# Low parts, copies and gate units of the first block given to other engines and places, and identity matmuls put ahead of five norms

## The chip, the cores and the metric

One core of a Trainium2 chip runs the whole program. The metric is device time in microseconds (us) for one execution, as the median of several runs. The engines are TensorE (PE in the profile; its weight loads are PEld), VectorE (DVE), ScalarE (ACT), GpSimd (POOL) and SyncE (SP), which here issues the DMAs of the weights. Each engine works through its own instructions in the order in which they stand in the program, and waits where an operand or a buffer is not ready.

## The reference

Input x is 256 rows of 1024 columns. A first block mixes the rows by three kinds of attention and a gated merge, and has a feed-forward part; two layers of a second block follow. What the change touches lies in the first block's mixing part and at the norms:

```python
h = rmsnorm(x, mix_norm_g[l])
proj = h @ w_in[l]
qa, ka, va, qd, kd, vd, qm, graw = jnp.split(proj, split_at, axis=-1)
heads = lambda t, n: t.reshape(B, S, n, HEAD_DIM)
qa = rope(rmsnorm(heads(qa, N_MOBA_HEADS), moba_q_norm_g[l]), positions)
ka = rope(rmsnorm(heads(ka, N_MOBA_HEADS), moba_k_norm_g[l]), positions)
...
gates = jax.nn.sigmoid(graw.astype(jnp.float32)).astype(x.dtype).reshape(B, S, N_BRANCHES, D_MODEL)
mem_n = rmsnorm(mem, mem_norm_g[l])
mkv = (mem_n @ w_mem_kv[l]).reshape(B, N_MEM, 2, N_MEM_HEADS, HEAD_DIM)
...
o_a = moba_attention(qa, ka, va).reshape(B, S, MOBA_W) @ w_branch_moba[l]
o_d = dilated_attention(qd, kd, vd).reshape(B, S, DIL_W) @ w_branch_dil[l]
o_m = memory_attention(qm, mk, mv).reshape(B, S, MEM_W) @ w_branch_mem[l]
merged = gates[:, :, 0] * o_a + gates[:, :, 1] * o_d + gates[:, :, 2] * o_m
x = x + merged @ w_out[l]
h2 = rmsnorm(x, ffn_norm_g[l])
...
```

Each layer of the second block has two more such norms, one ahead of its own input product and one ahead of the expert part: `h = rms_norm(x, norm1_g[l])` and `h2 = rms_norm(x, norm2_g[l])`.

## The kernel before

**Products.** Every large product is made of three: each operand is split into a high part, rounded to TensorE's fp32r format, and a low part, the rest; high x high, high x low and low x high are added up. `wload` (L88) brings one 128-row piece of a weight, a *unit*, into the chip: a DMA into `raw` (four buffers), a ScalarE copy that rounds it to `hi` (L102), and a subtraction that gives the *low part* `lw` (L103); `hi` and `lw` have three buffers each. On which engine the low part runs is set by `lo_on`: a pattern of engines, taken in turn, unit by unit. `gemm_n_unit` (L175 to L190) multiplies one unit: for each of the two halves t of the rows, L187 (high x high), L188 (high x low) and L190 (low x high). That is 12 matmuls of 128x512 for a unit of 1024 columns and 6 for one of 512. The sums stand in four accumulators `acc`; other results of TensorE go to four `tmp` buffers.

**Norms.** `norm_T` (L153) sums the squares of the rows, works out the factor of each row, scales the rows (L158 on ScalarE, L159 on VectorE), transposes them in 16 pieces of 128x128 on TensorE (L165) and splits each transposed tile (L111 on ScalarE, L112 on VectorE). Five norms come right behind a product whose sums they need: `ffn` in the first block (about 280 us), and `n1` and `n2` in either layer of the second (about 480, 615, 1435 and 1570 us). In these the first row of the list of products stands still until norm, transposes and first splits are done.

**The mixing part of the first block** runs from the start to 280 us. In the program's order:

- `w_in` in column groups for the heads, into `pj`, then the norm of `mem` and the product with `w_mem_kv` (eight units of 512 columns, low parts by turns on VectorE and GpSimd), into `kv`.
- `head_norm` and `rope_pair` on VectorE for the heads in `pj` (L429 to L452). `rope_pair` does, for each of two halves of the rows and two groups of six heads, six operations of 192 elements.
- The 24 units of the gates (three times 1024 columns, eight units each) are kept in a list `fill`. Two of them stand ahead of the first `head_T`, one is put behind each step of the attention rounds, and what is left stands at the end. All their low parts are on GpSimd (`lo_on(GP)`).
- `head_T` (L454) transposes the heads, four pieces to a `tmp` buffer (L460), and copies the result into `qkT`, by turns on ScalarE (L464) and VectorE (L466).
- The attention rounds (`run_pairs`, L296): scores (L233), a row maximum and a softmax on VectorE and ScalarE, transposes, products with the values.
- The branches: for each of three, a product of the attention's output with `w_branch` (3, 3 and 2 units), then for each quarter of the result a gated product on VectorE (L533) and, from the second branch on, an add into `merged` (L536). `merged` is transposed (L544), split, and multiplied with `w_out` (eight units). Low parts are on GpSimd here too.

A scheduler sets the order on each engine from the order in the code, with `high_priority` drawing instructions forward, and `tc.issue_after` holding one back until another has been issued.

## Time and profile before

| | |
|---|---|
| median of 3 runs | 2402.12 us (2401.92 to 2405.55) |
| profiled execution | 2397.52 us, its span 2395.7 us |
| TensorE busy | 2292.6 us, 96% of the span |
| VectorE busy | 1611.9 us, 67% |
| ScalarE busy | 1240.3 us, 52% |
| GpSimd busy | 675.1 us, 28% (275 of its 279 operations are low parts) |
| mean granted clock of TensorE | 0.974 of full speed |

In the rows further below, an operation is written as line, engine, kind, result <- operands, shape. Square brackets or the last column give the idle time of the engine ahead of it and what ended that. The granted clock is the share of TensorE's full speed (2.4 GHz) that it was given in a stretch; the values 0.50 and 0.51 are the lower level, 1.2 GHz.

### The profile page before, as it was taken

The page shows a single profiled execution, that of the slowest core. Times are in us where ns is not written, and L with a number is a line of the kernel's source. Part 1 is how long each engine was busy: PE and PEld are TensorE (multiplying, and loading weights), DVE is VectorE, ACT ScalarE, POOL GpSimd, SP SyncE. Part 2 cuts the span into 40 slices and gives each one's busy share as a digit, 9 for nine tenths or more (in the row PEclk, how much of TensorE's full clock was granted, in tenths as well). Part 3 has the DMA queues.
Part 4 walks back from the last instruction along what each step waited for, and adds up shares of the span by engine and source line. Part 5 has one row for each costly group of instructions (what it writes and reads, how often), then busy time and mean ns, then how long its engine had stood idle before and what let it go on. Part 6 is the DMA issues. An engine that isn't in the chain of part 4 may idle for free. (4 is left out here: it accounts for less than half of the span.)

```text
span 2395.7 us, 37317 instructions
## 1 busy us (share of the span) xinstructions
PE 2292.6 (96%) x13972; PEld 2000.6 (84%) x13972; DVE 1611.9 (67%) x3269; ACT 1240.3 (52%) x1997; POOL 675.1 (28%) x279
## 2 busy tenths in 40 slices
PE   7799899989999999999999998999999999999998
PEld 6578688777898999998888877889899999888886
DVE  7832577767597667776666667759766777666665
ACT  5444466545444555555555544544455555555553
POOL 3436444334576111220000004468512122000000
PEclk9899899989999999999999998999999999999999
DMA  6424355524454555446666653445455555666664
GB/s 205 137 80 149 130 181 192 168 86 136 158 168 151 167 160 176 165 162 194 193 194 193 194 175 94 136 157 169 151 166 160 167 174 163 192 194 194 193 193 149
DMA packets 111934, 393.07 MB, mean 164 GB/s; under 512 B 13432, under 2 KB 14328, under 8 KB 111496
## 3 DMA queue, kind: packets, MB, share of 16 engines
q1 hardware_dynamic: 108288, 384.42, 50.6%
q10 hardware_dynamic: 3464, 6.26, 0.8%
q8 instruction: 110, 1.80, 0.3%
q14 instruction: 72, 0.59, 0.1%
HBM read 389.58 MB, written 1.05 MB: 163 GB/s over the span
## 5 line engine op out<-in xcount | busy, mean ns | idle before, releaser
L103 POOL TENSOR_TENSOR lw<-raw,hi 128x1024 fp32r<-128x1024 f32 (+1 forms) x275 | 674.9, 2459 | 1357.5 <-ACT hi L102 1159.4
L102 ACT ACTIVATE hi<-raw 128x1024 fp32r<-128x1024 f32 (+1 forms) x748 | 778.0, 1040 | 442.5 <-PE tmp L205 188.1
L103 DVE TENSOR_TENSOR lw<-raw,hi 128x1024 fp32r<-128x1024 f32 (+2 forms) x473 | 573.2, 1214 | 219.0 <-ACT hi L102 218.5
L204 PE MATMUL tmp<-th,hi 128*128 128x256 f32 x1696 | 494.6, 292 | 5.2 <-DVE th L112 3.3
L206 PE MATMUL tmp<-th,lw 128*128 128x256 f32 x1696 | 484.3, 286 | 9.8 <-POOL lw L103 9.8
L187 PE MATMUL acc<-hi,th 128*128 128x512 f32 x1248 | 491.0, 394 | 2.7 <-ACT pj L374 2.4
L188 PE MATMUL acc<-lw,th 128*128 128x512 f32 x1248 | 490.2, 393 | 2.6 <-POOL lw L103 1.9
L205 PE MATMUL tmp<-th,hi 128*128 128x256 f32 x1696 | 483.8, 285 | 0.3
L213 PE MATMUL tmp<-th,hi 128*128 128x512 f32 x1136 | 411.4, 399 | 0.9 <-DVE th L112 0.9
L190 PE MATMUL acc<-hi,th 128*128 128x512 f32 x1248 | 393.4, 391 | 0.0
L206 PEld LDWEIGHTS tmp<-th,lw 128*128 128x128 f32 x1696 | 327.4, 193 | 11.1 <-POOL lw L103 10.6
L204 PEld LDWEIGHTS tmp<-th,hi 128*128 128x128 f32 x1696 | 327.6, 193 | 8.0 <-DVE th L112 5.0
L205 PEld LDWEIGHTS tmp<-th,hi 128*128 128x128 f32 x1696 | 328.0, 193 | 1.2 <-DVE th L112 0.7
L187 PEld LDWEIGHTS acc<-hi,th 128*128 128x128 f32 x1248 | 235.8, 189 | 53.6 <-ACT pj L374 2.8
L188 PEld LDWEIGHTS acc<-lw,th 128*128 128x128 f32 x1248 | 236.1, 189 | 53.1 <-POOL lw L103 2.7
L215 PE MATMUL tmp<-th,lw 128*128 128x256 f32 x994 | 279.8, 281 | 0.0
L190 PEld LDWEIGHTS acc<-hi,th 128*128 128x128 f32 x1248 | 235.5, 189 | 49.6 <-issue 0.7
L111 ACT ACTIVATE th<-W 128x256 fp32r<-128x256 f32 x252 | 104.4, 419 | 284.5 <-PE acc L188 284.5
L213 PEld LDWEIGHTS tmp<-th,hi 128*128 128x128 f32 x1136 | 213.2, 189 | 41.8 <-DVE th L112 1.3
L215 PEld LDWEIGHTS tmp<-th,lw 128*128 128x128 f32 x994 | 188.9, 190 | 1.9
L112 DVE SCALAR_TENSOR_TENSOR th<-W,th 128x256 fp32r<-128x256 f32 x252 | 106.2, 424 | 111.5 <-PE acc L190 111.4
L982 DVE TENSOR_TENSOR tmp<-tmp,pb 128x256 f32<-128x256 f32 x98 | 42.4, 432 | 150.2 <-ACT pb L981 149.9
(339 smaller groups left out, 2472.1 us busy)
## 6 DMA issues: line engine op xcount, KB each, us to landing
raw<-in_u_dram SPq DMA_DIRECT2D x256, 512.0 KB, 3.7
raw<-in_v_dram SPq DMA_DIRECT2D x256, 512.0 KB, 3.5
raw<-in_w_up_dram SPq DMA_DIRECT2D x44, 512.0 KB, 3.6
raw<-in_w_in_dram SPq DMA_DIRECT2D x40, 512.0 KB, 3.5
raw<-in_w2t_dram SPq DMA_DIRECT2D x32, 512.0 KB, 3.9
raw<-in_wq_dram SPq DMA_DIRECT2D x32, 512.0 KB, 3.5
raw<-in_w_out_dram SPq DMA_DIRECT2D x24, 512.0 KB, 3.4
raw<-in_w_down_dram SPq DMA_DIRECT2D x22, 512.0 KB, 3.6
```

The costliest lines, as they stand in the source:

```text
L102: SC.activation(hi[:, :ncols], r, AF.Copy)
L103: lo.tensor_sub(lw[:, :ncols], r, hi[:, :ncols].bitcast(F32))
L111: SC.activation(hi, ps, AF.Copy, scale=scale)
L112: V.scalar_tensor_tensor(lo, ps, scale, hi.bitcast(F32), op0=ALU.mult, op1=ALU.subtract)
L187: PE.matmul(ps, lh, wh[:, sl], start=first, stop=False)
L188: PE.matmul(ps, lh, wl[:, sl], start=False, stop=False)
L190: PE.matmul(ps, ll, wh[:, sl], start=False, stop=last)
L204: PE.matmul(ps, wh[:, sl], ah[:, c, :], start=(c == 0), stop=False)
L205: PE.matmul(ps, wh[:, sl], al[:, c, :], start=False, stop=False)
L206: PE.matmul(ps, wl[:, sl], ah[:, c, :], start=False, stop=(c == KC - 1))
L213: PE.matmul(ps, wh[:, sl], a2[:, c].rearrange("p a b -> p (a b)"), start=(c == 0), stop=(c == KC - 1))
L215: PE.matmul(ps[:, :S], wl[:, sl], a2[:, c, 0], start=False, stop=False)
```

## The change

1. `keep_going(n)` is new: n matmuls of the 128x128 identity with a 128x512 view of itself (bf16) into one `tmp` buffer, the first bound by `issue_after` to the last L190 of the product before. The five norms named above call it with 18. Nothing reads what they write.
2. Low parts: on VectorE alone for `w_mem_kv`, for the first six gate units, for the branches and for `w_out`; by turns on VectorE and GpSimd for the other gate units.
3. `rope_pair` takes both halves of the rows in one operation: six operations of 384 elements for each group of heads.
4. `head_T` copies on ScalarE alone.
5. Six gate units, not two, ahead of the first `head_T`.
6. The branches' adds come behind all four gated products of a branch, and each takes both halves of the rows (128x2x512).

```diff
--- before.py
+++ after.py
@@ -150,7 +150,17 @@
                 V.scalar_tensor_tensor(y, r, 1.5, y, op0=ALU.add, op1=ALU.mult)
         return [c[3] for c in cols], sq
 
-    def norm_T(src, scratch, g, hi, lo):
+    def keep_going(n):
+        ps = tmp_tile().rearrange("p (a b) -> p a b", a=4)
+        wide = identb[:, None].to_broadcast([128, 4, 128])
+        with tc.issue_after(hold["mm"].ins):
+            PE.matmul(ps, identb, wide, start=True, stop=True)
+        for _ in range(n - 1):
+            PE.matmul(ps, identb, wide, start=True, stop=True)
+
+    def norm_T(src, scratch, g, hi, lo, spins=0):
+        if spins:
+            keep_going(spins)
         with tc.high_priority(offset=150):
             rstd, sq = row_rstd(src, scratch)
             for h in range(2):
@@ -187,7 +197,7 @@
                     PE.matmul(ps, lh, wh[:, sl], start=first, stop=False)
                     PE.matmul(ps, lh, wl[:, sl], start=False, stop=False)
                 for ps, sl in grp:
-                    PE.matmul(ps, ll, wh[:, sl], start=False, stop=last)
+                    hold["mm"] = PE.matmul(ps, ll, wh[:, sl], start=False, stop=last)
 
     def gemm_n(units, ncols, ah, al, order=None, pre=()):
         nh = (ncols + 511) // 512
@@ -382,6 +392,7 @@
 
         mh = ab.tile([128, KC, S], F32R, name="mh", tag="mh")
         ml = ab.tile([128, KC, S], F32R, name="ml", tag="ml")
+        lo_on(V)
         norm_T(mem, xn, P("mem"), mh, ml)
         accs = gemm_n([A["w_mem_kv"][c * 128:(c + 1) * 128, :] for c in range(KC)], 512, mh, ml)
         evac_pj(accs, 0, 512, kv)
@@ -436,20 +447,19 @@
                 V.tensor_mul(v, v, rs[:, t, :nheads, None].to_broadcast([128, nheads, 64]))
 
         def rope_pair(c0, ty0):
-            for t in range(2):
-                for i in range(2):
-                    v = pj[:, t, c0 + i * 384:c0 + (i + 1) * 384].rearrange("p (h d) -> p h d", d=64)
-                    x1, x2 = v[:, :, :32], v[:, :, 32:]
-                    T = [tab[:, ty0 + i, k, t, None, :].to_broadcast([128, 6, 32]) for k in range(4)]
-                    ta = at.tile([128, 6, 32], F32, name="ta")
-                    tb = at.tile([128, 6, 32], F32, name="tb")
-                    tcc = at.tile([128, 6, 32], F32, name="tcc")
-                    V.tensor_mul(ta, x1, T[0])
-                    V.tensor_mul(tb, x2, T[1])
-                    V.tensor_mul(tcc, x1, T[2])
-                    V.tensor_mul(x2, x2, T[3])
-                    V.tensor_sub(x1, ta, tb)
-                    V.tensor_add(x2, tcc, x2)
+            for i in range(2):
+                v = pj[:, :, c0 + i * 384:c0 + (i + 1) * 384].rearrange("p t (h d) -> p t h d", d=64)
+                x1, x2 = v[:, :, :, :32], v[:, :, :, 32:]
+                T = [tab[:, ty0 + i, k, :, None, :].to_broadcast([128, 2, 6, 32]) for k in range(4)]
+                ta = ab.tile([128, 2, 6, 32], F32, name="ta")
+                tb = ab.tile([128, 2, 6, 32], F32, name="tb")
+                tcc = ab.tile([128, 2, 6, 32], F32, name="tcc")
+                V.tensor_mul(ta, x1, T[0])
+                V.tensor_mul(tb, x2, T[1])
+                V.tensor_mul(tcc, x1, T[2])
+                V.tensor_mul(x2, x2, T[3])
+                V.tensor_sub(x1, ta, tb)
+                V.tensor_add(x2, tcc, x2)
 
         def head_T(src, c0, w, s0):
             for c in range(0, w // 128, 2):
@@ -460,10 +470,7 @@
                         PE.transpose(ps[:, i * 256 + t * 128:i * 256 + (t + 1) * 128],
                                      src[:, t, c0 + (c + i) * 128:c0 + (c + i + 1) * 128], ident)
                 d = qkT[:, s0 + c:s0 + c + n, :].rearrange("p a b -> p (a b)")
-                if (c // 2) % 2 == 0:
-                    SC.copy(d, ps[:, :n * 256])
-                else:
-                    V.tensor_copy(d, ps[:, :n * 256])
+                SC.copy(d, ps[:, :n * 256])
 
         oh = ab.tile([128, KC, S], F32R, name="oh", tag="mh")
         ol = ab.tile([128, KC, S], F32R, name="ol", tag="ml")
@@ -493,10 +500,10 @@
             for _ in range(min(n, len(fill))):
                 fill.pop(0)()
 
-        lo_on(GP)
+        lo_on(V)
         head_norm(pj, 0, 12, "a")
         rope_pair(0, 0)
-        some_fill(2)
+        some_fill(6)
         head_T(pj, 0, 768, 0)
         head_norm(pj, 1152, 12, "d")
         rope_pair(1152, 2)
@@ -507,6 +514,7 @@
                          cmul=[ctab[:, 0, :128], ctab[:, 1, :]]) for hp in range(3)]
         mma = [attention(at, (2 * hp, 2 * hp + 1), qkf(12), qkf(14), vf(kv, 256), True,
                          (oh[:, 6 + hp, :], ol[:, 6 + hp, :])) for hp in range(2)]
+        lo_on(V, GP)
         run_pairs(moba[:2], fill, 1)
         head_T(pj, 1152, 768, 6)
         head_norm(pj, 2304, 4, "q")
@@ -522,6 +530,7 @@
         run_pairs(mma, fill, 1)
         some_fill(len(fill))
 
+        lo_on(V)
         merged = xn
         for b, (k0, kn) in enumerate([(0, 3), (3, 3), (6, 2)]):
             accs = gemm_n([A["w_branch"][(k0 + c) * 128:(k0 + c + 1) * 128, :] for c in range(kn)],
@@ -532,8 +541,11 @@
                     m = merged[:, t, h * 512:(h + 1) * 512]
                     V.scalar_tensor_tensor(m if b == 0 else g, g, 1.0, accs[t * 2 + h],
                                            op0=ALU.add, op1=ALU.mult)
-                    if b:
-                        V.tensor_add(m, m, g)
+            if b:
+                for h in range(2):
+                    sl = slice(b * 1024 + h * 512, b * 1024 + (h + 1) * 512)
+                    m = merged[:, :, h * 512:(h + 1) * 512]
+                    V.tensor_add(m, m, graw[:, :, sl])
         half = ab.tile([128, 1], F32)
         V.memset(half, 0.5)
         uh, ul = hT_tiles()
@@ -548,7 +560,7 @@
 
         fh, fl = hT_tiles()
         f2 = both[0]
-        norm_T(x, xn, P("ffn"), fh, fl)
+        norm_T(x, xn, P("ffn"), fh, fl, spins=18)
         lo_on(V, GP)
         accs = [acc_tile() for _ in range(4)]
 
@@ -624,7 +636,7 @@
             mh = ab.tile([128, KC, S], F32R)
             ml = ab.tile([128, KC, S], F32R)
             hh, hl = hT_tiles()
-            norm_T(x, xn, P(f"n1{l}"), hh, hl)
+            norm_T(x, xn, P(f"n1{l}"), hh, hl, spins=18)
 
             def proj_pair(i):
                 ps = tmp_tile()
@@ -875,7 +887,7 @@
 
             h2h, h2l = hT_tiles()
             h22 = both[0]
-            norm_T(x, carve(2, D), P(f"n2{l}"), h2h, h2l)
+            norm_T(x, carve(2, D), P(f"n2{l}"), h2h, h2l, spins=18)
             kt = carve(2, 8, 128)
             SC.dma_start(kt, A["kt"][l])
             sc = carve(8, 2, 2, 128)
```

Three places of the program, as the built kernels have them. First VectorE in the product with `w_mem_kv`, from the head norm's last multiplies on (`hrs` are the norm's factors, `ta`, `tb`, `tcc` and `tab` belong to the rope). Before:

```order
L436 TENSOR_TENSOR pj<-pj,hrs 128x768
L103 TENSOR_TENSOR lw<-raw,hi 128x512
L436 TENSOR_TENSOR pj<-pj,hrs 128x768
L447 TENSOR_TENSOR ta<-pj,tab 128x192
L448 TENSOR_TENSOR tb<-pj,tab 128x192
L449 TENSOR_TENSOR tcc<-pj,tab 128x192
L450 TENSOR_TENSOR pj<-pj,tab 128x6x32
L103 TENSOR_TENSOR lw<-raw,hi 128x512
L451 TENSOR_TENSOR pj<-ta,tb 128x6x32
L452 TENSOR_TENSOR pj<-tcc,pj 128x6x32
```

After:

```order
L447 TENSOR_TENSOR pj<-pj,hrs 128x768
L103 TENSOR_TENSOR lw<-raw,hi 128x512
L447 TENSOR_TENSOR pj<-pj,hrs 128x768
L103 TENSOR_TENSOR lw<-raw,hi 128x512
L457 TENSOR_TENSOR ta<-pj,tab 128x384
L103 TENSOR_TENSOR lw<-raw,hi 128x512
L458 TENSOR_TENSOR tb<-pj,tab 128x384
L459 TENSOR_TENSOR tcc<-pj,tab 128x384
L460 TENSOR_TENSOR pj<-pj,tab 128x2x6x32
L103 TENSOR_TENSOR lw<-raw,hi 128x512
L461 TENSOR_TENSOR pj<-ta,tb 128x2x6x32
L103 TENSOR_TENSOR lw<-raw,hi 128x512
```

Between the operations of the rope there now stand more low parts, and each operation of the rope takes both halves of the rows.

Second, TensorE ahead of the first scores (`th_129` is the normed input of the gates, `identb` and `trib` make the causal mask). Before:

```order
L188 MATMUL acc<-lw,th_129 128x512
L190 MATMUL acc<-hi,th_129 128x512 x2
L460 MATMUL tmp<-ident,pj 128x128 x10
L187 MATMUL acc<-hi,th_129 128x512
L188 MATMUL acc<-lw,th_129 128x512
L187 MATMUL acc<-hi,th_129 128x512
L233 MATMUL tmp<-qkT 128x128
L238 LDWEIGHTS identb
```

After:

```order
L198 MATMUL acc<-lw,th_129 128x512
L200 MATMUL acc<-hi,th_129 128x512 x2
L470 MATMUL tmp<-ident,pj 128x128 x10
L197 MATMUL acc<-hi,th_129 128x512
L198 MATMUL acc<-lw,th_129 128x512
L197 MATMUL acc<-hi,th_129 128x512
L198 MATMUL acc<-lw,th_129 128x512
L200 MATMUL acc<-hi,th_129 128x512
L243 MATMUL tmp<-qkT 128x128
L248 LDWEIGHTS identb
```

A half unit is five rows, of which each fence shows the last two. Ahead of the transposes of the heads (L460, now L470) stood two gate units, and now six. Between the transposes and the first scores there stand five products instead of three.

Third, VectorE from the third step of the second branch to the split of the merged rows, before:

```order
L533 SCALAR_TENSOR_TENSOR graw<-graw,acc 128x512 x2
L536 TENSOR_TENSOR xn<-xn,graw 128x512 x2
L533 SCALAR_TENSOR_TENSOR graw<-graw,acc 128x512 x2
L536 TENSOR_TENSOR xn<-xn,graw 128x512 x2
L533 SCALAR_TENSOR_TENSOR graw<-graw,acc 128x512 x2
L536 TENSOR_TENSOR xn<-xn,graw 128x512 x2
L112 SCALAR_TENSOR_TENSOR th_2028<-tmp,half,th_2028 128x2x256 x4
```

and after:

```order
L103 TENSOR_TENSOR lw<-raw,hi 128x1024
L542 SCALAR_TENSOR_TENSOR graw<-graw,acc 128x512 x3
L548 TENSOR_TENSOR xn<-xn,graw 128x2x512 x2
L542 SCALAR_TENSOR_TENSOR graw<-graw,acc 128x512 x4
L548 TENSOR_TENSOR xn<-xn,graw 128x2x512 x2
L103 TENSOR_TENSOR lw<-raw,hi 128x1024
L112 SCALAR_TENSOR_TENSOR th_1988<-tmp,half,th_1988 128x2x256 x4
L103 TENSOR_TENSOR lw<-raw,hi 128x1024 x7
```

The adds of a branch (L536, now L548) have moved behind all four of its gated products, and the low parts of `w_branch` and `w_out` stand in VectorE's order, the first of `w_out` behind the last adds, seven behind the splits. At the `ffn` norm TensorE has, ahead of the 16 transposes, the new matmuls in a row, the last of them between the third and the fourth group of four transposes.

## Rows read from the trace of the kernel before

**Rows 1.** Busy times in two stretches: length, PE, PEld, DVE, ACT, POOL, PEclk, DMA, GB/s.

```profile
66.00:98.00 32.00, 26.63 (x99) 20.11 (x99) 28.13 (x68) 14.61 (x23) 15.67 (x8) 0.89 0.48 158
126.00:220.00 94.00, 92.94 (x502) 74.60 (x501) 26.88 (x90) 44.49 (x91) 47.42 (x20) 0.98 0.34 105
```

**Rows 2.** Waits of TensorE, 56 to 290 us; columns: total us, times, longest.

```profile
PE tmp L233 <- DVE qkT L466: 7.4, 1, 7.4
...
PE acc L188 <- POOL lw L103: 3.8, 2, 3.2
...
PE acc L187 <- DVE graw L533: 3.2, 1, 3.2
...
PE acc L188 <- DVE lw L103: 2.1, 2, 1.6
```

**Rows 3.** TensorE in six stretches: length, busy, granted clock, DMA share, GB/s.

```profile
91.40:94.80 3.40, 3.40 (x9) 0.51 0.85 295
108.50:125.60 17.10, 12.06 (x31) 0.50 0.15 49
146.10:149.50 3.40, 3.40 (x9) 0.51 0.01 2
245.00:248.40 3.40, 3.40 (x10) 0.51 0.10 41
251.80:255.20 3.40, 1.40 (x13) 1.00 0.33 112
279.20:289.40 10.20, 7.29 (x27) 0.50 0.35 101
```

**Rows 4.** Timeline of VectorE in the memory product; columns: start, us from start to end.

```profile
81.10 0.34 DVE L450 TENSOR_TENSOR pj<-pj,tab 128x192 f32<-128x192 f32 x1
81.37 1.75 DVE L103 TENSOR_TENSOR lw<-raw,hi 128x512 fp32r<-128x512 f32 x1
...
85.19 0.68 DVE L103 TENSOR_TENSOR lw<-raw,hi 128x512 fp32r<-128x512 f32 x1
```

**Rows 5.** Timeline of GpSimd, 74 to 114 us; x2, x5: equal operations.

```profile
85.35 6.72 POOL L103 TENSOR_TENSOR lw<-raw,hi 128x512 fp32r<-128x512 f32 x2 [2.78 <-ACT hi L102]
96.42 12.50 POOL L103 TENSOR_TENSOR lw<-raw,hi 128x1024 fp32r<-128x1024 f32 x5 [4.36 <-ACT hi L102]
```

**Rows 6.** Timeline of VectorE ahead of the first scores.

```profile
96.44 5.20 DVE L436 TENSOR_TENSOR pj<-pj,hrs 128x256 f32<-128x256 f32 x2
...
111.36 0.76 DVE L436 TENSOR_TENSOR kv<-kv,hrs 128x256 f32<-128x256 f32 x2
```

**Rows 7.** Timeline of TensorE from the third branch to the ffn norm.

```profile
249.00 0.40 PE L188 MATMUL acc<-lw,oh 128*128 128x512 f32 x1
249.23 0.40 PE L190 MATMUL acc<-hi,ol 128*128 128x512 f32 x1
...
253.80 1.53 PE L544 MATMUL tmp<-ident,xn 128*128 128x128 f32 x12 [2.67 <-DVE xn L536]
...
281.26 3.68 PE L165 MATMUL tmp<-ident,xn 128*128 128x128 f32 x16 [4.07 <-ACT xn L158]
285.79 0.80 PE L213 MATMUL tmp<-th,hi 128*128 128x512 f32 x1 [0.85 <-DVE th L112]
```

**Rows 8.** Groups by shape, 56 to 300 us; columns: count, busy us, mean ns of one.

```profile
L103 DVE TENSOR_TENSOR lw<-raw,hi 128x1024 fp32r<-128x1024 f32 x4 | 4.9, 1216 | 1.2 <-ACT hi L102 1.2
...
L464 ACT COPY qkT<-tmp 128x512 f32<-128x512 f32 x6 | 3.1, 586 | 0.0
```

**Rows 9.** Timeline of VectorE in the branches.

```profile
238.19 4.89 DVE L536 TENSOR_TENSOR xn<-xn,graw 128x512 f32<-128x512 f32 x2
...
244.20 1.28 DVE L536 TENSOR_TENSOR xn<-xn,graw 128x512 f32<-128x512 f32 x2
```

**Rows 10.** Waits of TensorE from 300 us to the end.

```profile
PE tmp L165 <- ACT W L158: 8.4, 2, 4.2
PE tmp L165 <- ACT xn L158: 8.1, 2, 4.1
```

## The prediction

> **What bounds the kernel now.** I read the busy times by stretch first. In the attention stage TensorE is busy 92.94 of 94 us; in the stretch from 66 to 98 us it is busy only 26.63 of 32 at a mean clock of 0.89, and VectorE there 28.13 of 32 [rows 1]. So TensorE is the bound nearly everywhere, and time can be won only where it waits or runs at the lower of its two clock levels. TensorE's waits from 56 to 290 us, by what ended them, then show what is late: low parts (3.8 us behind GpSimd's, 2.1 behind VectorE's), a copy of transposed heads on VectorE (7.4), a gated product on VectorE (3.2) [rows 2]. Last I read the granted clock around each wait: after the wait for L188 it is 0.51 for 3.4 us, around the one at L233 0.50 for 17.1 us, after the one at the branches 0.51 for 3.4, around the ffn norm 0.50 for 10.2 [rows 3]. 0.5 is 1.2 GHz, and each us of TensorE work there costs half a us more than at 2.4 GHz.
>
> VectorE is late because of GpSimd. A 512-column low part on VectorE takes 0.68 us free and 1.75 beside one of GpSimd [rows 4], of which two take 6.72 us there [rows 5]; two 256-column multiplies take 5.20 us while five low parts run on GpSimd back to back, and 0.76 afterwards [rows 5, 6]. The change takes GpSimd out of these places.
>
> **The change, part by part.** All sums are differences against the profiled execution, 2397.52 us (span 2395.7 plus 1.8 around it). The median of the runs is 2402.12, 0.2% above; I take the same difference off the median.
>
> A. *Memory product, 512-column low parts all on VectorE, rope merged over t.* TensorE loses 3.8 + 2.1 us to late low parts, the longest being 3.2 and 1.6; the rest, 0.6 (the first gate unit) and 0.5 (ahead of the memory product), falls outside. So 4.8 of waiting lies inside, and 3.4 us at half clock, worth 1.7 [rows 2, 3]. In the new order VectorE does a low part, then one or two operations of head norm or rope. A unit of six products takes TensorE 6 x 0.23 = 1.4 us [rows 7]. VectorE needs 0.6 for the low part (0.68 less the overlap with the next operation), and a rope operation of 192 elements takes 0.34, the next operation starting 0.27 after it [rows 4]; merged ones of 384 I put at 0.47, worked out between the 0.27 spacing and the 0.68 of 512 columns. So 0.6 + 1.5 x 0.47 = 1.3 against 1.4: it just keeps up. 24 merged operations instead of 48 save 24 x 0.07 = 1.7 us of VectorE. I keep 1.0 us of new waiting at the start, where the queue of head-norm operations stands ahead. Gain 4.8 + 1.7 - 1.0 = **5.5** (bounds 3 and 6.5: over half of the old wait kept as VectorE's, or none).
>
> B. *Six gate units ahead of the heads' transposes, copies on ScalarE.* Before, two units are put there; TensorE then stands 7.4 us in L233 for VectorE's copy, which stands behind the 5.20 us multiplies and the key norms [rows 2, 6]. Now four more units, 4 x 12 x 0.23 = 11 us of products that were done after the last attention round anyway, stand in front, and the copy goes to ScalarE (0.59 us) [rows 8], where only hi copies of weights are queued. TensorE waits for the third copy at most, 0.8 us less the five products in between, so I keep 0.3. The six units' low parts on VectorE take 6 x 1.2 = 7.2 us [rows 8] in 16.4 us of products, beside the head norms; these end before the sixth unit does. Gain 7.4 + 0.4 (of the 0.6 at the first gate unit) - 0.3 = 7.5. The clock: 12.06 us of work at 0.50 would take 6.0 less; I keep one 3.4 us stretch at half, as there is one in mid-attention at 146 with nothing waiting ahead of it [rows 3], worth 1.7. Gain 4.3. The cover of later rounds: 24 units less 6 leave 18 for rounds that take 16 now as before, and the two left over stand ahead of branches whose heads are done. Together 11.8, of which I take **11**, since part of the 12.06 us may wait for softmax at full clock (bounds 6.5 and 13).
>
> In the rounds the low parts now alternate between VectorE and GpSimd: nine of 1.2 us go to an engine that is busy 26.88 of 94 us [rows 1]. Nothing is won, since TensorE is the bound there. A low part on VectorE that meets one of GpSimd can be held up by it, as 1.75 for 0.68 and 5.20 for 0.76 show [rows 4, 6]; I cost that at nothing, because a unit of 2.7 us covers a low part of 2.4, and price it as the fourth rival. The Trainium skill, page "SBUF — State Buffer", gives the reason: a VectorE operation with two SBUF operands and a GpSimd operation that reads SBUF take a shared port pair in turn, each for its whole instruction. By this rule, which these rows bear out, the alternating pattern works against the change, by up to 9 x 2.4 = 21.6 us if nothing covered it.
>
> C. *Branches: low parts on VectorE, adds after the gated products and over both t.* Now each gated product waits behind adds of 2.4 us each (4.89 for two) while GpSimd runs; free, two take 1.28 [rows 9]. TensorE waits 3.2 for its accumulator and then runs 3.4 us at half clock (1.7) [rows 2, 3]. In the new order all four gated products of a branch come ahead of the adds, and the next branch's low parts are done earlier still, so both go: 4.9. At the end, the last product is issued at 249.23 and the 12 last transposes start at 253.80 [rows 7], so the next product comes some 5.9 after it. Then: the last gated product is done at +1.0, the two wide adds take as long as a low part, 1.2 each [rows 8], eight transposes of 0.11 follow, together 4.3 to 4.4: gain 1.5. But w_out's first low part now stands behind the adds on VectorE and the second behind four splits; I charge 0.8 for the second, and 0.7 for a two in five chance that the clock falls in this pause. Gain 4.9 + 1.5 - 0.8 - 0.7 = **4.9** (bounds 2 and 6.4).
>
> D. *Identity matmuls ahead of five norms.* Before the ffn norm TensorE stands 4.07 us, then does 16 transposes in 3.68 and waits 0.85 more, the clock at 0.50 until 289.4 [rows 3, 7]; the pauses ahead of the other four norms are 4.1 to 4.2 long [rows 10]. 18 matmuls at the products' pace of 0.23 take 4.1 us: they fill the pause and end when the normed rows are ready. If the clock then stays up, the transposes take 2.0 (twelve took 1.53 at full clock [rows 7]), but the first product still waits for the splits, which run on ScalarE and VectorE as before, so only the products up to 289.4 gain, 3.6 / 2 = 1.8 less 0.4 for a start one split later: 1.4. I take 1.1 as a mean of five, 5.4 in all. But behind faster transposes TensorE stands some 2.7 us, and a pause of 3.2 did drop the clock [rows 2, 3], one of 2.67 did not [rows 7]. If it falls there, the site gives -0.3. At half of the sites: **2.5** (bounds -2.5, where all five fall and each row of 18 also ends 0.2 late, and 5.4).
>
> The Trainium skill, page "TensorE: Matmul & The Clock Gate", Part 4, says that the full clock does not engage for transposes; by it the clock would fall behind the spins at all five norms, and D would come to -1.5, as in the second rival. The trace speaks against it: from 251.8 to 255.2 TensorE did nothing but transposes, 1.40 us of 3.4, and the clock stayed at 1.00 [rows 3].
>
> Sum: 5.5 + 11 + 4.9 + 2.5 = 23.9. 2402.1 - 23.9 = **2378.2 us**.
>
> **The rivals.**
> 1. *VectorE becomes the bound ahead of the heads.* It was busy 28.13 of 32 us [rows 1] and gets four low parts more there and six after. If it does not keep up, A is 3 and B 6.5, sum 16.8: 2385. For: 1.3 against 1.4 is thin. Against: its own time shrinks where GpSimd stops.
> 2. *The clock falls at all five norms all the same*, behind the transposes: D is 5 x -0.3 = -1.5, sum 19.9: 2382. For: the fall behind the wait of 3.2 [rows 2, 3]. Against: the stretch at 251.8 [rows 3].
> 3. *Less is undone than read:* the heads' copy is only one of several things that are late at L233 (ScalarE's hi copies queue ahead of the copies), so a wait of some 5 us stays, the clock falls with it (4.3 lost), and C keeps its half clock. Sum 23.9 - 5 - 4.3 - 2 = 12.6: 2389.5.
> 4. *Slower.* In the nine rounds with a low part on VectorE, it meets a low part of GpSimd and is held up by up to 2.4 us; the softmax operations behind it in VectorE's order wait with it, TensorE runs through its one unit and stands, and the clock falls behind that as at 91.4. Price 2.4 plus 1.7 each, 9 x 4.1 = 37: 2415. It decides from 23.9 / 9 = 2.7 us a round. Against: VectorE is 71% idle there [rows 1], the two engines work on neighbouring units, a unit apart, and TensorE has that unit to do.
>
> **How the numbers follow.** Forecast 0.45; rival 1 0.20, rival 2 0.18, rival 3 0.12, rival 4 0.05. The forecast alone reaches from 2370 (A, B and C at nearly their upper bounds) to 2386. Down to the third rival it holds 0.95 less the tails; I set the range 2368 to 2390, which leaves out the slower rival and the edges. A measurement of this kernel can tell some 0.2%, 4.8 us. Faster by more: 0.90 (all of the first four cases less a tail), within 0.2%: 0.05, slower: 0.05.
>
> **What would show it.** Right: the wait at L233 (now L243) under 1.5 us and the granted clock 1.0 from 100 to 125 us but for one short stretch; the mem units without a wait over 1 us and no VectorE multiply over 1 us there; no wait for a gated product at the branches; each norm's pause filled with matmuls. Wrong: waits for VectorE's low parts in the memory product (rival 1), 0.5 stretches that start right behind the transposes of the norms (rival 2), waits on ScalarE copies at the first scores (rival 3), softmax waits in mid-attention (rival 4).

## The result and the profile after

The changed kernel takes 2374.16 us (median of 3 runs, 2372.94 to 2374.28) against 2402.12 before: ratio 0.988, 95% interval 0.9862 to 0.9898. Its profiled execution took 2372.94 us with a span of 2371.1, against 2397.52 and 2395.7, so the two traces differ by 24.6 us. The starts of the first product of each stage, read from TensorE's timelines, divide that:

| stage | before, us | after, us | difference | forecast |
|---|---|---|---|---|
| up to the memory product | 79.73 | 78.40 | -1.3 | 0 |
| memory product (part A) | 18.16 | 11.54 | -6.6 | -5.5 |
| gates and attention rounds (part B) | 124.10 | 114.64 | -9.5 | -11 |
| branches, up to the w_out product (part C) | 33.14 | 27.78 | -5.4 | -4.9 |
| from there to TensorE's end (part D) | 2131.53 | 2129.38 | -2.1 | -2.5 |
| sum | | | -24.9 | -23.9 |

The waits of TensorE after the change, from 30 to 290 us (total us, times, longest), answer to [rows 2]:

```profile
PE acc L198 <- DVE lw L103: 3.0, 3, 1.6
PE tmp L223 <- DVE th L112: 2.4, 1, 2.4
PE tmp L556 <- DVE xn L548: 2.0, 1, 2.0
...
PE tmp L175 <- ACT xn L168: 0.4, 1, 0.4
```

The 7.4 us at the first scores, the 3.8 for GpSimd's low parts and the 3.2 for an accumulator are gone. The transposes of the merged rows still wait for the adds (L556 <- L548), 2.0 us where it was 2.67 [rows 7]. The wait for the first split at the ffn norm (L223) has grown from 0.85 [rows 7] to 2.4. The two stretches of [rows 1] (length, PE, PEld, DVE, ACT, POOL, PEclk, DMA, GB/s) have become:

```profile
66.00:98.00 32.00, 30.57 (x128) 23.32 (x128) 28.82 (x70) 18.03 (x26) 3.87 (x3) 1.00 0.63 204
126.00:220.00 94.00, 92.98 (x486) 73.71 (x486) 43.54 (x103) 43.77 (x85) 19.14 (x8) 0.98 0.38 119
```

From 66 to 98 us TensorE is busy 30.57 us of 32, not 26.63, at the full clock. GpSimd works 3.87 us there, not 15.67, and VectorE hardly more than before, though it has more low parts to do. In the memory product (VectorE, start and length) nothing is stretched any more; compare [rows 4]:

```profile
78.46 0.55 DVE L457 TENSOR_TENSOR ta<-pj,tab 128x384 f32<-128x384 f32 x1
78.93 0.69 DVE L103 TENSOR_TENSOR lw<-raw,hi 128x512 fp32r<-128x512 f32 x1
79.53 0.56 DVE L458 TENSOR_TENSOR tb<-pj,tab 128x384 f32<-128x384 f32 x1
```

A merged rope operation takes 0.55 us, the next one starting 0.47 after it, and a low part 0.69.

At the ffn norm (TensorE; compare [rows 7]) the identity matmuls fill the pause, and a second one follows:

```profile
254.38 0.39 PE L157 MATMUL tmp<-identb 128*128 128x512 bf16 x1
254.61 3.62 PE L159 MATMUL tmp<-identb 128*128 128x512 bf16 x16
258.61 1.53 PE L175 MATMUL tmp<-ident,xn 128*128 128x128 f32 x12 [0.39 <-ACT xn L168]
259.98 0.38 PE L159 MATMUL tmp<-identb 128*128 128x512 bf16 x1
260.42 0.66 PE L175 MATMUL tmp<-ident,xn 128*128 128x128 f32 x4
263.47 0.80 PE L223 MATMUL tmp<-th,hi 128*128 128x512 f32 x1 [2.39 <-DVE th L112]
```

The granted clock (fourth number) in stretches of TensorE, answers to [rows 3]; all falls up to 270 us are among them, later ones but for 464.8 are left out:

```profile
109.80:113.20 3.40, 3.40 (x18) 1.00 0.80 276
113.20:120.00 6.80, 6.80 (x18) 0.50 0.01 2
161.00:164.40 3.40, 3.40 (x10) 0.50 0.11 46
229.20:232.60 3.40, 3.40 (x17) 0.50 0.03 12
263.40:266.80 3.40, 3.33 (x10) 0.50 0.89 278
464.80:468.20 3.40, 3.40 (x18) 0.51 0.26 98
```

TensorE at the end of the branches, from the transposes of the merged rows to w_out's first product (compare [rows 7]):

```profile
229.13 3.57 PE L556 MATMUL tmp<-ident,xn 128*128 128x128 f32 x16 [2.01 <-DVE xn L548]
232.36 0.61 PE L197 MATMUL acc<-hi,th 128*128 128x512 f32 x1
```

### The profile page after: what moved, and what is told of

The parts are those of the page before. It is cut to its first block, busy times and chain, and to the rows that moved or that the text cites. A ratio compares the mean times of both kernels' runs of the same rounds, so it can differ in the third digit from the quotient of the medians.

```text
span 2371.1 us, 37461 instructions
## 1 busy us (share of the span) xinstructions
PE 2298.0 (97%) x14062; PEld 1996.1 (84%) x14062; DVE 1629.9 (69%) x3274; ACT 1240.3 (52%) x1999; POOL 587.4 (25%) x244
## 4 chain that ended last, share of the span: by engine, by line
PE 88%; DVE 6%; issue 2%; ACT 2%; POOL 2%; DMA 1%; ACTq 0%; DVEq 0%; POOLq 0%
PE acc L198 13%; PE acc L200 13%; PE acc L197 13%; PE tmp L223 11%; PE tmp L214 9%; PE tmp L216 8%; PE tmp L215 8%; PE tmp L225 5%; PE acc L1047 3%; POOL lw L103 2%; DVE lw L103 1%; PE tmp L243 1%; PE tmp L297 1%; PE tmp L222 1%; DVE x L232 1%
## 5 line engine op out<-in xcount | busy, mean ns | idle before, releaser
L103 POOL TENSOR_TENSOR lw<-raw,hi 128x1024 fp32r<-128x1024 f32 (+1 forms) x240 | 587.2, 2451 | 1420.2 <-ACT hi L102 815.9
L103 DVE TENSOR_TENSOR lw<-raw,hi 128x1024 fp32r<-128x1024 f32 (+2 forms) x508 | 617.4, 1217 | 242.5 <-ACT hi L102 242.2
L223 PE MATMUL tmp<-th,hi 128*128 128x512 f32 x1136 | 411.8, 400 | 2.4 <-DVE th L112 2.4
L225 PE MATMUL tmp<-th,lw 128*128 128x256 f32 x994 | 279.9, 282 | 0.0
L223 PEld LDWEIGHTS tmp<-th,hi 128*128 128x128 f32 x1136 | 213.6, 189 | 43.4 <-DVE th L112 2.6
```

What stands on the lines that cost most here:

```text
L103: lo.tensor_sub(lw[:, :ncols], r, hi[:, :ncols].bitcast(F32))
L223: PE.matmul(ps, wh[:, sl], a2[:, c].rearrange("p a b -> p (a b)"), start=(c == 0), stop=(c == KC - 1))
L225: PE.matmul(ps[:, :S], wl[:, sl], a2[:, c, 0], start=False, stop=False)
```

## Experiments

In each run the kernel before ran on the same chip; ratios are against that. The 95% intervals reach some 0.2% to either side, about 5 us, so parts of 2 us can't be told apart by ratios; the stage times of the traces do that. One caution goes with them. The run without the identity matmuls (e2, below) has the same instructions in the same order as the changed kernel up to the ffn norm, and yet its gates and rounds took 118.1 us against 114.6: it has a stretch at half clock at 140.7 us that the other lacks, and one of 6.8 us at 161 against 3.4. Its six runs lie between 2372.41 and 2378.74. So what a stage with attention rounds takes differs by some 3.5 us from one execution to the next. The branches differ too: e1 (below) has the instructions of the kernel before up to the ffn norm, and its branches took 35.3 us against 33.1, its rounds 126.4 against 124.1.

### What the early gate units, the copies and the gates' low parts are worth (part B)

Theory, as predicted: six units cover VectorE's work ahead of the first scores. Rival: it is enough that the copies stand on an engine that isn't late. The six units, the copies and the pattern of low parts in the rounds were each undone alone, then all of it together with the low parts of the first units, which were not undone alone.

e6_two_early:

```diff
-        some_fill(6)
+        some_fill(2)
```

> The changed kernel with two gate units, not six, ahead of the first transposes of heads; copies stay on ScalarE. Theory 1 (the six units cover VectorE's work that the scores wait for): a wait of 4 us or more at the first scores and a longer half-clock stretch, 7 to 11 us above the changed kernel. Theory 2 (the copy's engine is what mattered: on ScalarE it stands behind no head norm): the wait at the first scores is under 1.5 us and the time within 2 us of the changed kernel.

Measured: 2372.74 us (2369.67 to 2376.0), ratio 0.9884 (0.9864 to 0.9905). The scores begin at 98.37 us, without a wait, and the time is not above the changed kernel's: the rival holds.

e7_copies_by_turns:

```diff
-                SC.copy(d, ps[:, :n * 256])
+                if (c // 2) % 2 == 0:
+                    SC.copy(d, ps[:, :n * 256])
+                else:
+                    V.tensor_copy(d, ps[:, :n * 256])
```

> The changed kernel with the heads' copies by turns on ScalarE and VectorE as before; six early gate units stay. Theory 1 (six units cover VectorE's work): VectorE's copy is done when the scores come, no wait over 1 us there, within 1.5 us of the changed kernel. Theory 2 (the copy's engine mattered): a wait of 3 us or more at the first scores, 3 to 8 us above.

Measured: 2376.36 us (2373.75 to 2379.35), ratio 0.9904 (0.9887 to 0.9921). No wait at the first scores either. The time is 2.2 us above the changed kernel's, which the ratios can't tell; the rounds took 117.5 us, with the clock at half for 17 us in three stretches as in e2.

e8_gates_gp:

```diff
-        lo_on(V, GP)
+        lo_on(GP)
         run_pairs(moba[:2], fill, 1)
```

> The changed kernel with the low parts of the gate units in the attention rounds all on GpSimd. Theory (TensorE is the bound in the rounds, so the engine of the low parts there gives nothing): within 1.5 us of the changed kernel. Rival 1 (alternating makes the two engines stop each other, as in the prediction's fourth rival): 2 us or more below the changed kernel. Rival 2 (GpSimd's 2.4 us a unit are too slow): 2 us or more above, with waits for low parts in the rounds.

Measured: 2377.17 us (2375.71 to 2378.74), ratio 0.9908 (0.9892 to 0.9925): 3.0 us above the changed kernel, by the time alone the second rival. The rounds took 117.5 us, with a half-clock stretch at 140.3 as in e2, and their only waits are two of 0.7 us or less for a softmax (L265); no wait for a low part of GpSimd is there. That speaks for the theory, and the 3 us lie within what two executions of the same rounds differ by. So the pattern in the rounds is not shown to give anything.

e12_b_undone, all of it, with the first units' low parts on GpSimd again:

```diff
-                SC.copy(d, ps[:, :n * 256])
+                if (c // 2) % 2 == 0:
+                    SC.copy(d, ps[:, :n * 256])
+                else:
+                    V.tensor_copy(d, ps[:, :n * 256])
...
-        lo_on(V)
+        lo_on(GP)
         head_norm(pj, 0, 12, "a")
...
-        some_fill(6)
+        some_fill(2)
...
-        lo_on(V, GP)
         run_pairs(moba[:2], fill, 1)
```

> The changed kernel with all of the second part of the change undone at once: two early gate units, heads' copies by turns on ScalarE and VectorE, low parts of all gate units on GpSimd. Each of these alone, undone, left no wait at the first scores. Theory 1 (they stand in for one another: any one of them takes VectorE's copy out from behind the multiplies that GpSimd holds up): the wait of some 7 us at the first scores and a half-clock stretch of 10 us or more are back, 7 to 11 us above the changed kernel. Theory 2 (VectorE is early enough at the first scores without them, since the memory product and the rope no longer hold it up): the wait is under 3 us and the time within 4 us of the changed kernel.

Measured: 2386.17 us (2384.39 to 2389.5), ratio 0.9936 (0.9918 to 0.9953), 12 us above the changed kernel. Its waits of TensorE (30 to 262 us), the clock there, GpSimd and VectorE (start, length):

```profile
PE tmp L243 <- DVE qkT L476: 10.4, 1, 10.4
```

```profile
100.90:121.40 20.50, 12.11 (x31) 0.50 0.12 37
```

```profile
89.11 11.76 POOL L103 TENSOR_TENSOR lw<-raw,hi 128x1024 fp32r<-128x1024 f32 x5 [14.05 <-ACT hi L102]
```

```profile
89.30 2.22 DVE L441 TENSOR_SCALAR hss<-hss 128x8 f32<-128x8 f32 x1
91.55 2.33 DVE L119 TENSOR_SCALAR hrs<-hss 128x24 int32<-128x24 int32 x1
...
104.53 0.17 DVE L441 TENSOR_SCALAR hss<-hss 128x8 f32<-128x8 f32 x1
104.73 0.18 DVE L119 TENSOR_SCALAR hrs<-hss 128x24 int32<-128x24 int32 x1
...
107.11 0.76 DVE L447 TENSOR_TENSOR kv<-kv,hrs 128x256 f32<-128x256 f32 x2
...
108.46 0.68 DVE L476 COPY qkT<-tmp 128x512 f32<-128x512 f32 x1
```

The wait is back, at 10.4 us, with 20.5 us at half clock. While five low parts run on GpSimd, two operations on 8 and 24 columns take 2.22 and 2.33 us on VectorE, and the copy for the scores comes at 108.46, behind all of the head norms. So the block is worth 12 us, more than the 7 to 11 that I expected for the first theory. By e6 and e7, neither the six units nor the copies' engine is needed while the rest stands. The expectation says that each part had been undone alone; that is not so for the low parts of the first units: in e8 these stayed on VectorE. That putting them on GpSimd again is by itself enough to bring the wait back is a rival that no run rules out, and the rows above, with VectorE held up while GpSimd does five of them, speak for it. I had credited the six units.

### What holds the memory product up (part A)

e5_mem_by_turns:

```diff
-        lo_on(V)
         norm_T(mem, xn, P("mem"), mh, ml)
```

> The changed kernel with the low parts of the memory product by turns on VectorE and GpSimd as before. Theory 1 (GpSimd's low parts there hold VectorE and TensorE up): waits of 1.6 and 3.2 us for low parts and a half-clock stretch are back in the memory product, and the time is 5 to 7 us above the changed kernel. Theory 2 (the merged rope is what made VectorE keep up): at most 2 us above.

Measured: 2376.43 us (2376.12 to 2376.81), ratio 0.9896 (0.9877 to 0.9915). The memory product takes 13.98 us: 11.54 in the changed kernel, 18.16 before. TensorE's waits in it (79.9 to 94 us):

```profile
PE acc L198 <- DVE lw L103: 2.2, 2, 1.8
```

```profile
81.33 1.43 POOL L103 TENSOR_TENSOR lw<-raw,hi 128x512 fp32r<-128x512 f32 x1 [3.28 <-ACT hi L102]
83.64 1.60 POOL L103 TENSOR_TENSOR lw<-raw,hi 128x512 fp32r<-128x512 f32 x1 [0.89 <-ACT hi L102]
88.49 1.40 POOL L103 TENSOR_TENSOR lw<-raw,hi 128x512 fp32r<-128x512 f32 x1 [3.25 <-ACT hi L102]
```

Against the first theory, the half-clock stretch did not come back, and GpSimd's low parts take 1.4 to 1.6 us there, not two in 6.72 [rows 5]. Moving the low parts is worth 2.4 of the 6.6 us, and some more ahead of the product: there TensorE waits 1.16 us for a low part on VectorE (at 78.65 us) that it does not wait for in the changed kernel, and the product starts at 79.93 us, not 78.40. By the time, 2.3 us above the changed kernel, the run lies next to the second theory. The other 4.2 stay with the other edits; the merged rope is the one that works in this stretch, but it was not run alone, so that it is the cause is argued and not shown.

### Order or engine in the branches (part C)

e3_old_adds:

```diff
-            if b:
-                for h in range(2):
-                    sl = slice(b * 1024 + h * 512, b * 1024 + (h + 1) * 512)
-                    m = merged[:, :, h * 512:(h + 1) * 512]
-                    V.tensor_add(m, m, graw[:, :, sl])
+                    if b:
+                        V.tensor_add(m, m, g)
```

> The changed kernel with the branches' adds as before: eight of 128x512, each right behind its gated product; low parts stay on VectorE. Theory 1 (the adds were slow only because GpSimd ran low parts beside them): an add takes 0.65 us, TensorE does not wait for an accumulator in the third branch, and the time is that of the changed kernel within 1.5 us. Theory 2 (the place of the adds ahead of the next gated products is what made TensorE wait): the wait for an accumulator is back with 1 us or more, and the time is 3 to 5 us above the changed kernel.

Measured: 2371.93 us (2369.49 to 2375.1), ratio 0.9873 (0.9852 to 0.9894). From the first branch product to w_out's takes 25.89 us, 1.9 less than with the wide adds.

e4_branch_gp:

```diff
-        lo_on(V)
+        lo_on(GP)
         merged = xn
```

> The changed kernel with the low parts of the branches and of w_out on GpSimd as before; the wide adds behind all four gated products stay. Theory 1 (GpSimd beside the adds is the cause): the adds of 128x2x512 stretch to 2.4 us or more, but no accumulator hangs on them any more, so only the last two count: the merged rows are transposed up to 2.5 us later, against which w_out's first low parts no longer stand on VectorE; 1 to 3 us above the changed kernel. Theory 2 (order alone): the same as the changed kernel within 1 us.

Measured: 2377.05 us (2374.09 to 2379.99), ratio 0.9899 (0.9877 to 0.9921); the branches take 31.29 us, 3.5 more than in the changed kernel. VectorE in the two (first e3, then e4; wide adds are L548, the old ones L545), and TensorE's waits from 200 to 262 us in e3 and in e4:

```profile
225.40 1.28 DVE L545 TENSOR_TENSOR xn<-xn,graw 128x512 f32<-128x512 f32 x2
...
227.80 1.28 DVE L545 TENSOR_TENSOR xn<-xn,graw 128x512 f32<-128x512 f32 x2
...
230.20 1.28 DVE L545 TENSOR_TENSOR xn<-xn,graw 128x512 f32<-128x512 f32 x2
```

```profile
221.96 4.62 DVE L548 TENSOR_TENSOR xn<-xn,graw 128x1024 f32<-128x1024 f32 x2
226.51 2.47 DVE L542 SCALAR_TENSOR_TENSOR graw<-graw,acc 128x512 f32<-128x512 f32 x4
228.90 4.44 DVE L548 TENSOR_TENSOR xn<-xn,graw 128x1024 f32<-128x1024 f32 x2
```

```profile
PE tmp L553 <- DVE xn L545: 1.3, 1, 1.3
PE acc L198 <- DVE lw L103: 0.7, 1, 0.7
PE acc L197 <- ACT th L111: 0.5, 1, 0.5
```

```profile
PE tmp L556 <- DVE xn L548: 5.4, 1, 5.4
```

No wait for a gated product is left in either. Taking GpSimd away (e3) or moving the adds (e4) each ends the wait of 3.2 us; but with GpSimd the wide adds take 2.3 us each and the transposes wait 5.4. Without GpSimd the order is not shown to matter. In the old one the last add is short and stands alone, so the transposes wait 1.3, not 2.0. But w_out's product then waits 0.7 for a low part and 0.5 for a split (the last two of e3's waits), and from its first matmul to TensorE's end e3 takes 2131.0 us, against 2129.4 in the changed kernel. Nor does the old order account for the half-clock stretch that e3 lacks: e5, e9, e11 and e12 have the wide adds and the wait of 2.0 and lack it too, and their branches take 26.5 us.

### The identity matmuls (part D)

e1_spins_only, the kernel before with nothing but these:

```diff
+    def keep_going(n):
+        ...
-        norm_T(x, xn, P("ffn"), fh, fl)
+        norm_T(x, xn, P("ffn"), fh, fl, spins=18)
...
```

> The kernel before with the identity matmuls of the five norms and nothing else of the change. Theory (the matmuls fill the pause of 4.1 us, but TensorE then stands again until the first splits are done, and the clock falls there at about half of the sites): 2.5 us faster than before, between 0 and 5.4; in the trace five rows of 18 matmuls that end within 0.5 us of the normed rows, a wait of 1.4 to 2.4 us behind the transposes, and at two or three of the five norms a stretch at half clock that begins behind the transposes. Rival (the clock falls at all five all the same): 1.5 us slower than before and half-clock stretches at all five. Second rival (the matmuls run late and hold the transposes up): the wait for the normed rows is gone, but the transposes start later than 4.1 us after the last product, and the time is 2 us or more above before.

Measured: 2398.08 us (2396.89 to 2403.83, 12 runs) against 2400.37 (17 runs), ratio 0.9987 (0.9975 to 0.9999). Its one trace is longer than that of the kernel before, 2397.1 us against 2395.7, by the rounds and branches ahead of the norms (see the caution above).

e2_no_spins, the changed kernel without them:

```diff
-        norm_T(x, xn, P("ffn"), fh, fl, spins=18)
+        norm_T(x, xn, P("ffn"), fh, fl)
...
```

> The changed kernel without the identity matmuls. Theory: 2.5 us slower than the changed kernel (about 2376.7 against 2374.2), with the pauses of 4.1 us and half-clock stretches of 6.8 to 10.2 us back at the five norms. Rival (the matmuls give nothing or cost): the same or up to 1.5 us faster than the changed kernel.

Measured: 2375.46 us (2372.41 to 2378.74), ratio 0.9884 (0.9864 to 0.9904); by ratios it can't be told from the changed kernel. From the first w_out product to TensorE's end, where alone the two differ, it takes 2131.8 us against 2129.4, so 2.4 us more; e1 takes 2128.9 there and the kernel before 2131.5, 2.7 less. The two agree with the forecast of 2.5. Ten traces have the 18 matmuls and no more, and take 2128.7 to 2131.0 us there, six of them 2129.5 or less; the two without take 2131.5 and 2131.8. So some 2 us are shown. The clock fell behind the transposes at two of the five norms (263.4 and 464.8 us), not at all.

e10_after_transposes puts 8 more behind the last transpose, where TensorE stands 2.4 us:

```diff
-                        PE.transpose(ps[:, c2 * 256 + t * 128:c2 * 256 + (t + 1) * 128],
+                        tr = PE.transpose(ps[:, c2 * 256 + t * 128:c2 * 256 + (t + 1) * 128],
...
+            if spins:
+                pa = acc_tile().rearrange("p (a b) -> p a b", a=4)
+                wide = identb[:, None].to_broadcast([128, 4, 128])
+                with tc.issue_after(tr.ins):
+                    PE.matmul(pa, identb, wide, start=True, stop=True)
+                for _ in range(7):
+                    PE.matmul(pa, identb, wide, start=True, stop=True)
```

> The changed kernel, with 8 more identity matmuls at each of the five norms, bound to the last transpose, into an accumulator buffer. They take 8 x 0.23 = 1.8 us and stand in waits of 2.4 us (ffn, n1) and 1.4 (n2). Theory (the second pause is what lets the clock fall at the ffn norm and at the first n1): the half-clock stretches right behind the transposes there go, worth 1.7 us each, less 0.4 at each of the two n2 where the matmuls overshoot: 2.5 us below the changed kernel. Rival (the falls do not hang on that pause): same or 1 us above.

Measured: 2366.79 us (2365.01 to 2371.88), ratio 0.9852 (0.983 to 0.9875). TensorE at the ffn norm, and the clock behind the ffn norm and the first n1:

```profile
260.40 0.38 PE L184 MATMUL acc<-identb 128*128 128x512 bf16 x1
260.62 1.67 PE L186 MATMUL acc<-identb 128*128 128x512 bf16 x7
262.96 0.50 PE L230 MATMUL tmp<-th,hi 128*128 128x512 f32 x1 [0.67 <-DVE th L112]
```

```profile
262.90:266.30 3.40, 3.34 (x19) 1.00 0.87 283
460.70:464.10 3.40, 3.33 (x27) 1.00 0.24 42
```

The wait is 0.67 us, the first product starts no later, and both falls are gone. From w_out's first product to the end it takes 2124.9 us, 4.5 less than the changed kernel and nearly twice the 2.5 expected; e11 below, with the same addition, takes 2125.1. The two falls that I had in view are not all that went: later in the ffn product TensorE runs at 1.00 from 279.9 to 283.3 us, where it ran at 0.50 from 280.4 to 283.8, and two stretches of 6.8 us at half (567.1 and 1519.5 us in the changed kernel) are down to 3.4. Why these went is open. The 8 were run only on top of the 18; what they would give alone no run shows.

### A clock that falls without a wait

e9_unit_between_scores:

```diff
-    def run_pairs(gens, fill, per, ahead=None):
+    def run_pairs(gens, fill, per, ahead=None, mid=0):
...
             for g in list(live):
+                if mid and fill and g is gens[-1]:
+                    mid -= 1
+                    fill.pop(0)()
...
-        run_pairs(moba[:2], fill, 1)
+        run_pairs(moba[:2], fill, 1, mid=1)
...
-        run_pairs(dil[1:], fill, 1)
+        run_pairs(dil[1:], fill, 1, mid=1)
```

> The changed kernel, with a gate unit put between the scores of the first and of the second pair of heads in the first and in the third call of the attention rounds (the two units that were left over at the end go there). In the changed kernel the clock falls to half at 113.2 us for 6.8 us and at 161.0 for 3.4, with no wait ahead of either: TensorE did nothing but scores there. Theory (a long row of score matmuls lets the clock fall): the falls at these two places go or shrink, and the time is 2 to 5 us below the changed kernel. Rival (the fall has another cause, or the wait for the last softmax, that the two units covered, comes back): the falls stay, the time is the same or up to 3 us above.

Measured: 2371.68 us (2369.93 to 2373.48), ratio 0.9873 (0.9848 to 0.9897). TensorE in the places of the two falls, and where one is now:

```profile
112.40:119.20 6.80, 6.80 (x33) 1.00 0.05 18
137.40:144.20 6.80, 6.80 (x19) 0.50 0.15 58
160.50:164.00 3.50, 3.50 (x16) 1.00 0.24 57
```

Both falls are gone, but another of 6.8 us stands at 137.4, in a call of the rounds that was left alone. The trace is 3.0 us shorter, of which 1.7 lie in the rounds and 1.3 in the branches, where nothing was edited; the ratio can't show that much. And the unit is not the only thing that decides: e3 has the changed kernel's instructions there, the same unbroken row of scores, and ran at 1.00 from 113.7 to 120.5 us, with 6.8 us at half from 136.8 and again from 160.7. In all, the clock fell in the first scores in eight of the nine traces with that row unbroken and no wait ahead of it, and in neither of the two with the unit (e9, e11). So the unit is likely to help at its place. The rounds took 113.0 us in e9 and 112.1 in e11, against 114.3 to 118.2 in the six traces with the changed kernel's rounds: two traces below a scatter that is wider than their lead.

e11_both has this and e10's addition (its edit is the two diffs above together).

> The changed kernel with a gate unit between the first scores in two calls of the rounds and with 8 identity matmuls behind the transposes of the five norms, the two additions that were tried one by one. If they add up (2.5 and 7.4 us in the medians): 2364 to 2366, about 1.5% below the kernel before. If they work on the same thing or hinder each other: 2367 or more.

Measured: 2364.81 us (2364.1 to 2367.52), ratio 0.9857 (0.984 to 0.9873). It has the lowest median of all and its trace is 7.6 us shorter than the changed kernel's. By the ratio it is not told apart from e10. The median lies within the 2364 to 2366 expected if the two add up.

## Why the prediction was right, step by step

- **The sum** was 23.9 against 24.9 in the traces. In the medians it is 28.0: the profiled execution of the kernel before lies 4.6 us below its median, that of the changed kernel 1.2 below, and I had carried the difference over unchanged. That the sum is off by only 1.0 is in part luck: errors of either sign cancel in it, and with rounds as in e2's trace B would have come to 6.0 and the sum to 21. Three side sums were off as well: D's terms make 2.0 at half of the sites, not 2.5 (then 23.4 in all), the first rival's sum is 16.9, and the forecast's lower end of 2370 takes the upper bound of D too.
- **A** was mis-sized by the 1.0 us of new waiting that I kept: in the memory product there is none. VectorE keeps up as worked out (0.47 from one rope operation to the next, as estimated). But e5 shows that the low parts' engine gives 2.4 us of it, not all. A further 1.3 were won ahead of the product, where TensorE's wait of 2.4 us for an accumulator's copy on ScalarE shrank to 0.6 and the clock no longer falls behind it; two waits for VectorE's low parts, together under 3.0 us, take part of that back. That the change ended this fall is not shown: e1 has the instructions of the kernel before there, and its wait is 1.1 and its clock 1.00.
- **B** came to 9.5 where its terms made 11.8 and I took 11. The wait at the first scores went as forecast: TensorE's idle time in the part fell from 9.0 to 1.2 us, 7.8 where the terms made 7.5. The step that was mis-sized is the clock. The sum left two stretches of 3.4 us at half, the old one at 146 us and a new one, worth 3.4 us together; there are 6.8 us at 113.2 and 3.4 at 161, worth 5.1. So the clock gave 2.6 us, from 7.7 lost to 5.1, and not 4.3. The reason that I gave for the wait's end, four more units, is not the needed one: e6 has no wait with two. Which part of the block is needed, the engine of the first units' low parts above all, the runs do not take apart.
- **C** was 4.9 against 5.4. The accumulator's wait went; e3 and e4 show that either half of the edit ends it. The 0.8 for w_out's second low part was not paid: there is no wait for it. The chance of a fall in the pause, counted at 0.7, became a fall at 229.2. So the pause from the last branch product to w_out's first, 5.9 us before and 4.3 to 4.4 forecast, is 5.63; in e5, e9, e11 and e12, where the clock does not fall there, it is the 4.36 that was worked out. Six of the ten traces with these adds and low parts on VectorE have the fall, all after the same wait of 2.0.
- **D** was 2.5 against 2.1 in the trace and 2.4 to 2.7 in e2 and e1; by its own terms, two falls at five sites make 2.7. The matmuls come every 0.23 us, and what is left of the wait is 0.39 at the ffn norm. Behind the transposes TensorE stands 2.4 us (2.7 forecast).
- **The clock at transposes.** The Trainium skill, page "TensorE: Matmul & The Clock Gate", Part 4, says that the full clock does not engage for transposes. If that decided it here, all five norms would fall, and two of five did; so no run here bears the rule out as a rule for this kernel. Nor does the length of the pause alone sort the falls, as the prediction's 3.2 against 2.67 suggests: in the kernel before, the clock fell at 67.5 us behind a wait of 2.40.
- **The rivals.** VectorE did not become the bound (0.2 us of waiting for its low parts from 78 to 130 us). Alternating low parts in the rounds did no harm: GpSimd's low parts there take 2.4 us as ever, and e8 without the alternation is not faster. Of the third rival, the wait at the scores is gone; the half clock in the branches is there, at 229.2, but behind another wait than the one meant.

## What to carry to other kernels

Before crediting an edit with a wait that it ends, undo it alone and then with the others that touch the same wait: here one wait of 7 to 10 us had several edits against it, two of which could each be left out, and the one that no run left out alone (the first units' low parts) may be the one that counts. When two engines slow each other, look first at which of the two can be taken out of the stretch: in the branches either that or the order of the adds ended the wait of 3.2 us, and GpSimd's low parts left in cost 3.5 us there all the same. A pause filled ahead of a chain may come back behind its next step, so fill that as well: in the traces 8 matmuls behind the transposes, added to the 18 ahead of them, gave more (4.5 us) than the 18 had given (2.4 to 2.7). And run the same instructions twice before reading a stage's time to a microsecond.

## What the runs showed of the hardware that I had not expected

- The clock fell with TensorE busy all the time: from 109.8 to 113.2 us it was busy 3.40 of 3.40 us at 1.00, on nothing but scores (64x128 and 64x256 operands) and their masks, and from 113.2 it ran at 0.50 for 6.8 us. With a gate unit between the two groups of scores (e9) it kept 1.00 there, but so it did in e3 without one.
- One-operand operations on 8 and 24 columns took 2.22 and 2.33 us on VectorE beside GpSimd's low parts, and 0.17 to 0.18 where GpSimd stood still: here small operations of a chain paid nearly as much as large ones (two multiplies of 128x256 took 5.20 [rows 6]).
- Two executions with the same instructions up to the ffn norm (the changed kernel and e2) differ by 3.4 us ahead of it: the clock is at half for 10.2 us of the attention rounds in one and for 17 in the other.
